# One projection of a hybrid decoder step: the prompt's mLSTM over five tiles, and six tiles as pairs

## The chip, the cores and the metric

The kernel runs on one core of a Trainium2 chip. A core has a matrix engine (TensorE, in the profile PE, with its weight loads as PEld), a vector engine (VectorE, DVE), a scalar engine (ScalarE, ACT), GpSimd (POOL) and a queue engine (SyncE, SP) that issues most of the transfers; POOL issues some as well. Matrix products go to PSUM, which has eight banks, and DVE or ACT must take them out. The metric is the device time of one execution in microseconds.

## What is computed

The reference is one inference step of a hybrid decoder layer. A prompt of 512 tokens and 32 sample tokens (8 sequences of 4), 544 columns in all, pass an input projection; an mLSTM branch and a windowed attention branch work side by side; each has its own output projection, gated; the sum goes through w_out and a layer norm with a residual. Cut to what matters here:

```python
q_m, k_m, v_m, o_m, z_m, q_a, k_a, v_a, z_a, g_m, g_a, i_pre, f_pre = split(x @ w_in)
# mLSTM of the prompt, 4 heads of 512: decays d from the gates, and
s = einsum('bhtd,bhsd->bhts', q, k) * d                  # cells
h = s @ v / max(|den|, exp(-m_row))                      # then a norm over the head, times the gates
C_new = decay * C + einsum('bhsk,bhsv->bhkv', w * k, v)  # keys: the new matrix memory, and n alike
# windowed attention with sinks gives the branch b_a, mLSTM the branch b_m (2048 wide each)
y = sigmoid(g_m) * (b_m @ w_proj_m) + sigmoid(g_a) * (b_a @ w_proj_a)
out = layernorm(alpha * x + y @ w_out)
```

All products are done at float32 accuracy in three products of rounded parts: a = ah + al, b = bh + bl, and ab is taken as ah bh + ah bl + al bh. The parts are made by `split` for weights (a cast on ACT to `wh`, a subtraction on DVE to `wl`) and `hilo` for activations (the same two steps, any tile).

## The kernel before

A projection of 2048 by 2048 is worked in 16 column tiles of 128. There are two forms.

*Plain tile* (`gemm`, matmuls on L210): the weights of a tile come in two halves of 8 x 128 x 128 (512 KB each), each half is split, and 2 x 8 x 3 matmuls of 128x272 for each of two banks, 96 in all, make the tile. After every `every`-th of the 16 row blocks `tick()` lets each live generator go one step, so that other work is put in the order between the matmuls: with `every=2` a tile holds 8 ticks. `drain()` runs what generators are left to their end.

*Pair* (`paired`, matmuls on L685 and L687): two column tiles as one product of 2 x 2 blocks with seven half products of 24 matmuls of 128x272 in place of eight (Strassen's scheme in Winograd's form). It needs sums of weight halves (`prepare`: DVE additions, or with `acc` two of them as transfers from POOL that accumulate) and sums of the activations' blocks (n2, s1, s4, n3), which must be there before the half product that uses them: half products 0 to 6 use, in this order, the plain left block, s1, n2, the low block, n3, s4, the low block again.

The program goes through these stages: the input projection in pairs (to 1757 us in the profiled execution), beside it attention and the sample tokens; the attention branch's projection w_proj_a, 16 plain tiles; w_proj_m as 4 plain tiles, 5 pairs, 2 plain tiles; w_out as 4 plain tiles, pairs and a tail with the layer norm.

The prompt's mLSTM stands beside w_proj_a. It is a generator (`mlstm`) of 20 steps a head for four heads. In a head: `values` (transposes of v on PE, `vh` by ACT, `vl` by DVE; four times), `decays` (one product, two copies and ten exponentials on ACT, spawned beside it), `keys` (transposes on L1425, a gated key on DVE at L1427, its parts `kwh` and `kwl`, then 24 products of 128x258 on L1438, and copies of C to the output on L1441 and L1442; four times), `cells` (scores on L1470, times decays on L1473, their parts, products on L1483, the norm), and the output (transposes on L1493, gate products on L1494, stores to `d_brm`). The parts of k are made on DVE (L1519 and L1520). At 8 ticks a tile the four heads take some ten tiles. When the generator has ended, `branch(d_brm)` reloads and splits the mLSTM branch over the remaining tiles.

`operand_sums` makes the four activation sums of a projection that is to be done in pairs: 8 steps, each with one transfer of 544 KB from POOL into one of two buffers `tx`, four sums on DVE (L1587 to L1590) and four `hilo`. It runs beside the four plain tiles of w_proj_m and of w_out.

What sets the order: each engine runs its instructions in the order in which the program leaves them, and waits at the first whose operands are not there. The program's order is that of the code, except that `tc.high_priority(offset=...)` moves work forward by so many instructions, that `tc.issue_after(x)` holds work behind instruction x, and that work whose buffers come free early may be placed early. Buffers come from pools with a fixed count: PSUM has the pools psB (tag sm, four banks: mLSTM and the other small work) and psA (tag bank, four banks: the tiles). The SBUF pools carry `reuse_waits="tile"`, so that memory given to a new pool waits for each old tile in it by itself.

## Time and profile before

| | |
|---|---|
| time, median of 3 executions | 2467.47 us (2466.90 to 2468.39) |
| the profiled execution | 2464.16 us, span 2462.4 us |
| PE busy | 2433.8 us (99%), 19446 matmuls |
| DVE busy | 1884.0 us (77%), 2813 instructions |
| ACT busy | 1215.4 us (49%) |
| POOL busy | 509.9 us (21%) |
| DMA | 464.72 MB, mean 189 GB/s |

Durations and counts are those of the profiled execution. A busy share is a mean over all stages. A group of instructions is a line, an engine, an operation and its tiles (out<-in), with the count, the busy time, the mean ns of one, and the time for which the engine was idle before them with what ended it. The durations of neighbouring instructions of one engine overlap, so one that reads 0.68 us can be started every 0.60 us. A line of the waits is engine, tile and line, what it waited for, the sum in us, the times and the longest.

### The profile page before, as it was taken

How to read it: one execution, taken by the hardware profiler on the slowest of the kernel's cores; microseconds unless marked ns; L12 is line 12 of the kernel's file. 1: busy time of each engine (PE TensorE's matmuls, PEld its weight loads, DVE VectorE, ACT ScalarE, POOL GpSimd, SP SyncE). 2: the span in 40 equal slices, each digit the busy share in tenths (PEclk: the TensorE clock that was granted, in tenths of full speed). 3: DMA queues.
4: the chain of work that ended last, by engine and by line, in shares of the span. 5: the costliest groups of instructions: out<-in, count | busy, mean ns of one | idle time of the engine just before them, and what ended most of it. 6: DMA issues, size and time to landing. Idle time of an engine off the chain costs nothing.

```text
span 2462.4 us, 48812 instructions
## 1 busy us (share of the span) xinstructions
PE 2433.8 (99%) x19446; PEld 2378.9 (97%) x19446; DVE 1884.0 (77%) x2813; ACT 1215.4 (49%) x1994; POOL 509.9 (21%) x478
## 2 busy tenths in 40 slices
PE   8999999999999999999999999999999999999997
PEld 8999999999999999999999999999999999999996
DVE  7768888888888887787887888878855654767657
ACT  5456676676676564433433444544633333344431
POOL 3114334334333331211121122210000000110111
PEclk9999999999999999999999999999999999999998
DMA  6866666666666644578587687576755546888876
GB/s 177 201 173 158 163 161 144 162 161 150 160 154 160 155 124 138 143 217 247 179 242 244 163 241 229 176 251 217 246 171 173 187 147 210 226 218 253 220 221 188
DMA packets 557436, 464.72 MB, mean 189 GB/s; under 512 B 45592, under 2 KB 454344, under 8 KB 556952
## 3 DMA queue, kind: packets, MB, share of 16 engines
q1 hardware_dynamic: 540312, 402.09, 55.1%
q0 software_dynamic: 15696, 57.15, 12.1%
q8 instruction: 153, 2.51, 0.4%
q10 hardware_dynamic: 1200, 2.36, 0.3%
q14 instruction: 75, 0.61, 0.1%
HBM read 319.06 MB, written 96.31 MB: 169 GB/s over the span
## 4 chain that ended last, share of the span: by engine, by line
PE 94%; DMA 3%; DVE 2%; issue 1%; ACT 1%; SPq 0%; DVEq 0%; POOL 0%; ACTq 0%; POOLq 0%
PE bank L685 46%; PE bank L687 23%; PE bank L210 11%; PE sm L1438 2%; PE sm L210 1%; PE bank L1250 1%; PE sm L1470 1%; PE sm L795 1%; PE sm L1483 1%; PE sm L841 1%; DMA tx<-d_y 1%; DMA ty<-d_y 1%; DMA raw<-in_w_in 1%; PE sm L1800 1%; PE sm L821 1%
## 5 line engine op out<-in xcount | busy, mean ns | idle before, releaser
L200 ACT CAST wh<-raw 128x1024 fp32r<-128x1024 f32 x632 | 662.7, 1049 | 836.2 <-PE bank L685 686.6
L201 DVE TENSOR_TENSOR wl<-raw,wh 128x1024 fp32r<-128x1024 f32 x632 | 792.2, 1255 | 194.6 <-ACT wh L200 175.3
L685 PE MATMUL bank<-xk,wh 128*128 128x272 f32 x2336 | 322.7, 289 | 0.0
L665 DVE TENSOR_TENSOR raw<-raw,raw 128x1024 f32<-128x1024 f32 x238 | 304.1, 1279 | 12.6 <-DMA raw<-in_w_in 8.3
L685 PEld LDWEIGHTS bank<-xk,wh 128*128 128x128 f32 x2336 | 303.0, 188 | 2.8 <-issue 2.4
L704 POOL TENSOR_TENSOR ev<-p,ev 128x272 f32<-128x272 f32 x82 | 117.9, 1438 | 458.3 <-ACT ev L703 401.2
L685 PE MATMUL bank<-n2h,wh 128*128 128x272 f32 x656 | 169.8, 291 | 0.2 <-ACT wh L200 0.2
L687 PE MATMUL bank<-xk,wl 128*128 128x272 f32 x1168 | 169.7, 288 | 0.0
L685 PE MATMUL bank<-n3h,wh 128*128 128x272 f32 x656 | 169.6, 291 | 0.0
L685 PE MATMUL bank<-s1h,wh 128*128 128x272 f32 x656 | 169.1, 291 | 0.0
L685 PE MATMUL bank<-n2l,wh 128*128 128x272 f32 x656 | 167.7, 288 | 0.0
L685 PE MATMUL bank<-n3l,wh 128*128 128x272 f32 x656 | 167.6, 288 | 0.0
L685 PE MATMUL bank<-s1l,wh 128*128 128x272 f32 x656 | 167.3, 287 | 0.0
L685 PE MATMUL bank<-s4h,wh 128*128 128x272 f32 x656 | 167.2, 289 | 0.0
L685 PE MATMUL bank<-s4l,wh 128*128 128x272 f32 x656 | 167.0, 287 | 0.0
L687 PEld LDWEIGHTS bank<-xk,wl 128*128 128x128 f32 x1168 | 155.6, 188 | 0.1
L685 PE MATMUL bank<-a11h,wh 128*128 128x272 f32 x584 | 150.6, 290 | 0.0
L685 PE MATMUL bank<-a11l,wh 128*128 128x272 f32 x584 | 149.4, 288 | 0.0
L210 PE MATMUL bank<-bh,wl 128*128 128x272 f32 x704 | 147.5, 290 | 0.7 <-DVE wl L201 0.7
L210 PE MATMUL bank<-bh,wh 128*128 128x272 f32 x704 | 148.1, 289 | 0.0
L210 PE MATMUL bank<-bl,wh 128*128 128x272 f32 x704 | 148.0, 289 | 0.0
L663 POOL DMA_DIRECT2D raw<-raw x90 | 78.1, 868 | 291.8 <-DVE ev L712 202.2
(493 smaller groups left out, 5670.4 us busy)
## 6 DMA issues: line engine op xcount, KB each, us to landing
raw<-in_w_in SPq DMA_DIRECT2D x296, 512.0 KB
raw<-raw POOLq DMA_DIRECT2D x90, 512.0 KB, 4.8
C<-in_state_mlstm_C SPq DMA_DIRECT2D x32, 1024.0 KB
out<-C SPq DMA_DIRECT2D x64, 512.0 KB
raw<-in_w_proj_a SPq DMA_DIRECT2D x32, 512.0 KB
raw<-in_w_proj_m SPq DMA_DIRECT2D x32, 512.0 KB
raw<-in_w_out SPq DMA_DIRECT2D x32, 512.0 KB
d_v<-ev SPq DMA_DIRECT2D x16, 272.0 KB
```

The lines of the kernel that those rows point to most:

```text
L200: state["cast"] = A.copy(wh[:, k:k + n], raw[:, k:k + n])
L201: state["split"] = V.tensor_tensor(out=wl[:, k:k + n], in0=raw[:, k:k + n], in1=r32(wh[:, k:k + n]), op=ALU.subtract)
L210: PE.matmul(ps[f][:, :w], a[:, kk], b(k, c, w), start=(k == 0 and n == 0), stop=(k == 15 and n == 2))
L663: G.dma_start(out=w[out][:], in_=w[b][:], accum_op=ALU.add)
L665: V.tensor_tensor(out=w[out][:], in0=w[a][:], in1=w[b][:], op=ALU.add)
L685: PE.matmul(ps, wh[:, k], x(p, k), start=(first and k == 0 and p == 0), stop=False, skip_group_check=True)
L687: state["end"] = PE.matmul(ps, wl[:, k], x(0, k), start=False, stop=(k == 7), skip_group_check=True)
L704: G.tensor_tensor(out=c22, in0=p1, in1=c11, op=ALU.subtract)
L795: PE.matmul(pp[:, c0 + w0:c0 + 256], qs[a][:, j * 128:j * 128 + 128], kx[:, k0:k0 + 256 - w0], start=(n == 0), stop=(n == 1))
L821: PE.transpose(pt[:, b * 128:b * 128 + 128], s_[:, b, 128:256], ident)
L841: PE.matmul(po[:, b * 128:b * 128 + n], VA[:, b], p_[:, 2 * b:2 * b + n // 128], start=(b == 0 and m == 0), stop=(b == 3 and m == 1), skip ...
L1438: PE.matmul(pp[:, 0:258], a[:, b * 128:b * 128 + 128], b_[:, b, f], start=(b == 0 and n == 0), stop=(b == 3 and n == 2))
```

## The change

The line numbers of the new kernel differ: `gemm`'s matmuls are L216 there, the pairs' L691 and L693, `split` L206 and L207, `hilo` L251 and L252, the keys' transposes L1437, the gated key L1439, the keys' products L1450, the copies of C L1453 and L1454, scores L1482, the cells' products L1498, transposes and gate products of the output L1512 and L1513, the plain tile's eviction L1621, the loads of sums L1583 and L1584, the sums L1594 to L1600.

- The attention branch's projection has five plain tiles with the mLSTM beside them (`LEAD_A`), then three plain tiles with the operand sums of this branch beside them, then three pairs (tiles 8 to 13), then two plain tiles with `branch(d_brm)`.
- In the five tiles a half has other tick counts (`every=(1, 2)`: 12 ticks a tile), and the tiles' work is held behind the last matmul of the mLSTM put down so far (`behind_cells`). The mLSTM has 15 steps a head: the loads of k and v of the next head come a head earlier, the parts of q are made between the keys, and the output of a head (`rows_out`) is a generator of its own that runs beside the next head.
- The casts of k go from DVE to ACT (`two_parts` with `hilo`), and so does the second half of the copy of C.
- The PSUM pools also have `reuse_waits="tile"` and can be closed: six banks for sm and two for bank from the lead stage to the pairs, four and four before and after.
- `operand_sums` works in two passes of 8 steps, first n2 and s1, then s4 and n3, with two transfers a step (272 KB and 136 KB) into one of three buffers `tx`. All three projections use it; `rest` puts what is left of it ahead of the fifth half product of the first pair.

```diff
             kw["side"] = side or "right"
+        if space is not bass.MemoryType.DRAM:
             kw["reuse_waits"] = "tile"
...
+    esPS = ExitStack()
+    es.callback(esPS.close)
+
+    def psum_pools(n):
+        return pool(esPS, nm("psB"), n, PSUM), pool(esPS, nm("psA"), 8 - n, PSUM)
...
-            products(ps, half, wh, wl, xh, xl, cols, every)
+            products(ps, half, wh, wl, xh, xl, cols, every[half] if isinstance(every, tuple) else every)
...
-    def paired(work, plain=None):
+    def paired(work, plain=None, rest=()):
...
+            if at == 4:
+                for _ in rest:
+                    pass
...
+    esPS.close()
+    psB, psA = psum_pools(6)
...
-                    PE.matmul(pp[:, 0:258], a[:, b * 128:b * 128 + 128], b_[:, b, f],
+                    state["cells"] = PE.matmul(pp[:, 0:258], a[:, b * 128:b * 128 + 128], b_[:, b, f],
...
-        V.tensor_copy(co[:, 256:512], p1[:, 0:256])
+        A.copy(co[:, 256:512], p1[:, 0:256])
...
+        if h + 1 < MH:
+            pre["v"] = load4(d_v, h + 1)
+        gt = load4(d_g, h)
...
-            yield
-        gt = load4(d_g, h)
+            if js[-1] == 3 and h + 1 < MH:
+                pre["k"] = load4(d_k, h + 1)
+            yield
+        spawn(rows_out(h, hns, gt))
+
+    def rows_out(h, hns, gt):
         for c in range(4):
...
+        pre = {"v": load4(d_v, 0), "k": load4(d_k, 0)}
         for h in range(MH):
-            vts = load4(d_v, h)
+            vts, kts = pre["v"], pre["k"]
             spawn(decays(h))
-            yield
-            kts = load4(d_k, h)
             for c in range(4):
                 yield from values(h, c, vts[c])
             qts = load4(d_q, h)
             kh, kl, qh, ql = [], [], [], []
+
+            def two_parts(src, to):
+                a, b_ = t5(F32R), t5(F32R)
+                hilo(src[:], a[:], b_[:])
+                for tiles, t_ in zip(to, (a, b_)):
+                    tiles.append(t_)
+
             g_ = None
             for c in range(4):
-                a, b_ = t5(F32R), t5(F32R)
-                V.tensor_copy(a[:], kts[c][:])
-                V.tensor_tensor(out=b_[:], in0=kts[c][:], in1=r32(a[:]), op=ALU.subtract)
-                kh.append(a)
-                kl.append(b_)
+                two_parts(kts[c], (kh, kl))
                 n_ = keys(h, c, kts[c])
                 next(n_)
+                if c > 1:
+                    two_parts(qts[c - 2], (qh, ql))
                 if g_ is not None:
                     for _ in g_:
                         pass
                 g_ = n_
                 yield
-            for c in range(4):
-                a, b_ = t5(F32R), t5(F32R)
-                hilo(qts[c][:], a[:], b_[:])
-                qh.append(a)
-                ql.append(b_)
+            for c in (2, 3):
+                two_parts(qts[c], (qh, ql))
             for _ in g_:
                 pass
             yield
-            yield from cells(h, kh, kl, qh, ql)
+            yield from cells(h, kh, kl, qh, ql, pre)
...
+    def operand_sums(src, to, p, pace=1):
+        f, e = ([[p.tile([128, 4, 2, HT], F32R, tag="act", name=nm("sum" + n)) for _ in range(2)] for n in "hl"]
+                for _ in range(2))
+        to["n2"], to["s1"], to["s4"], to["n3"] = (
+            (lambda q, k, t=t, j=j: t[q][k // 4][:, k % 4, j]) for t in (e, f) for j in range(2))
+
+        def load(n):
+            k, c = n % 8, slice(HT, T) if n < 8 else slice(0, HT)
+            t_ = tx.tile([128, 3, HT], F32, tag="tx", name=nm("tx"))
+            G.dma_start(out=t_[:, 0:2].rearrange("p c t -> p (c t)"), in_=src[k])
+            G.dma_start(out=t_[:, 2], in_=src[k + 8][:, c])
+            return t_
+
+        ahead = [load(n) for n in range(3)]
+        for n in range(16):
+            for _ in range(pace if n < 12 else 1):
+                yield
+            k, t_ = n % 8, ahead.pop(0)
+            u, v, w = (t_[:, j] for j in range(3))
+            if n < 8:
+                V.tensor_tensor(out=v, in0=w, in1=v, op=ALU.subtract)
+                V.tensor_tensor(out=u, in0=u, in1=v, op=ALU.subtract)
+                to_ = e
+            else:
+                V.scalar_tensor_tensor(v, u, -1.0, v, op0=ALU.mult, op1=ALU.subtract)
+                V.tensor_tensor(out=u, in0=w, in1=r32(to["n2"](0, k)), op=ALU.subtract)
+                V.tensor_tensor(out=u, in0=u, in1=r32(to["n2"](1, k)), op=ALU.subtract)
+                to_ = f
+            hilo(t_[:, 0:2], *(t[k // 4][:, k % 4] for t in to_))
+            if n + 3 < 16:
+                ahead.append(load(n + 3))
...
+    def plain_a(ct, **kw):
         sg = c5t()
-        nc.sync.dma_start(sg[:], d_sga[ct])
-        ps = gemm(wa_, ct * 128, bah, bal, every=2)
+        with tc.issue_after(state["load"].ins):
+            nc.sync.dma_start(sg[:], d_sga[ct])
+        ps = gemm(wa_, ct * 128, bah, bal, **kw)
...
+        return dict(wv=wa_, x=XA, cA=ct * 128, cB=ct * 128 + 128, scale=1.0, acc=True, end=end, early=early)
+
+    LEAD_A, PAIR_A, TAIL_A = 5, 8, 14
+    def behind_cells():
+        return tc.issue_after(state["cells"].ins) if "cells" in state else ExitStack()
+
+    for ct in range(LEAD_A):
+        with behind_cells():
+            plain_a(ct, every=(1, 2))
     drain()
-    def operand_sums(src, to, p):
-
-        def load(k):
-            t_ = tx.tile([128, 2, T], F32, tag="tx", name=nm("tx"))
-            G.dma_start(out=t_[:], in_=src[k:k + 9:8].rearrange("k p t -> p k t"))
-            return t_
-
-        ahead = [load(0), load(1)]
-        for k in range(8):
-            for _ in range(2):
-                yield
-            t_ = ahead.pop(0)
-            r11, r21, r12, r22 = (t_[:, a, c:c + HT] for a in range(2) for c in (0, HT))
-            V.tensor_tensor(out=r22, in0=r22, in1=r21, op=ALU.subtract)
-            V.scalar_tensor_tensor(r21, r11, -1.0, r21, op0=ALU.mult, op1=ALU.subtract)
-            V.tensor_tensor(out=r11, in0=r11, in1=r22, op=ALU.subtract)
-            V.tensor_tensor(out=r12, in0=r12, in1=r11, op=ALU.subtract)
-            for name, r_ in (("s1", r22), ("n2", r11), ("n3", r21), ("s4", r12)):
-                if name not in to:
-                    to[name] = quad(p, name)
-                hilo(r_, to[name][0][:, k], to[name][1][:, k])
-            if k < 6:
-                ahead.append(load(k + 2))
-
-    def operands(tiles, sums):
-
-        low = [t[2:] for t in tiles]
-        return [side_by_side(tiles, 0), quarter(sums["s1"]), quarter(sums["n2"]), side_by_side(low, 0),
-                quarter(sums["n3"]), quarter(sums["s4"]), side_by_side(low, HT)]
-
-    def c6t():
-        return c6.tile([128, T], F32, tag="c6", name=nm("c6"))
+    esA.close()
+    es3, esE = ExitStack(), ExitStack()
+    act3 = pool(es3, "act3", 8)
+    c6 = pool(esE, "c6", 2)
+    esR = ExitStack()
+    wr2, pe_ = pool(esR, "wr2b", 3), pool(esR, "peb", 1)
+    tx = pool(esR, "txb", 3)
+    SA = {}
+    sums_ = operand_sums(d_bra, SA, act3, 2)
+    next(sums_)
+    spawn(sums_)
+    for ct in range(LEAD_A, PAIR_A):
+        with behind_cells():
+            plain_a(ct, every=2, prio=AHEAD)
+    esPS.close()
+    psB, psA = psum_pools(4)
+    XA = operands((bah_, bal_), SA)
+    paired([pair_a(ct) for ct in range(PAIR_A, TAIL_A, 2)], state["split"], rest=sums_)
+    state["end"] = None
+    drain()
+    bm_, bmh, bml, g_ = branch(d_brm, act3, lambda k: ev() if k % 5 < 3 else c6t())
+    spawn(g_)
+    for ct in range(TAIL_A, 16):
+        plain_a(ct, every=2, prio=AHEAD)
...
-    spawn(operand_sums(d_brm, M, act))
+    sums_ = operand_sums(d_brm, M, act)
+    next(sums_)
+    spawn(sums_)
```

## The prediction

> **What bounds the kernel now.** I read the page's busy table and slices first, then the windows of the stages that the change touches, then PE's own waits and the chain.

> ```profile
> span 2462.4 us, 48812 instructions
> PE 2433.8 (99%) x19446; PEld 2378.9 (97%) x19446; DVE 1884.0 (77%) x2813; ACT 1215.4 (49%) x1994; POOL 509.9 (21%) x478
> PE   8999999999999999999999999999999999999997
> ...
> 1740.00:1760.00 20.00, 19.30 (x154) 19.08 (x153) 16.02 (x22) 13.97 (x21) 1.47 (x1) 1.00 1.01 332
> 1760.00:1780.00 20.00, 20.00 (x165) 19.95 (x164) 18.70 (x31) 14.99 (x30) 0.21 (x2) 1.00 0.81 262
> 1780.00:1800.00 20.00, 20.00 (x153) 19.53 (x153) 7.57 (x16) 3.90 (x8) 0.00 (x0) 1.00 0.35 111
> 2020.00:2120.00 100.00, 100.00 (x804) 100.00 (x803) 58.40 (x104) 36.88 (x62) 4.35 (x6) 1.00 0.74 225
> ...
> PE bank L210 <- DVE wl L201: 1.5, 2, 0.7
> ...
> 2014.15 111.71 PE bank L210 x895
> ```

> The columns of a window are its length, the busy time of PE, PEld, DVE, ACT and POOL, the granted clock, the DMA share and GB/s. PE is dense: its only wait from 1757 to 2400 is one of 0.70 us (the waits list it twice). So PE's work sets the time: work taken from PE is gained in full, and every wait that PE gets is paid in full. DVE has idle time on average, but at the start of the first mLSTM head (1760 to 1780) it is busy 18.70 of 20 us and ACT 14.99. This is the stage that the change compresses.

> **The sum's base.** The profiled execution took 2464.16 us (span 2462.4), 3.3 us below the median 2467.47. I sum against it and add 3.3 at the end.

> **What PE loses.** Six tiles of the projection become three pairs, with seven half products of 24 matmuls each where two tiles had eight: 3 x 24 = 72 matmuls of 128x272 go, and all other PE work stays. The chain's row gives 111.71 / 895 = 0.1248 us for one, so PE has 9.0 us less work: -9.0.

> **What is packed.** The same mLSTM now stands beside five tiles, not ten, so some 60 us less of matmuls cover it, and the operand sums of this branch are new work. I counted PE's work through the new order of instructions, in us t from the first product of w_proj_a (t = 0 is 1757.7 in this trace), and laid DVE's and ACT's queues beside it in their new order, with these durations:

> ```profile
> L201 DVE TENSOR_TENSOR wl<-raw,wh 128x1024 fp32r<-128x1024 f32 x21 | 25.6, 1218 | 4.8 <-ACT wh L200 4.7
> L200 ACT CAST wh<-raw 128x1024 fp32r<-128x1024 f32 x21 | 22.1, 1050 | 19.4 <-issue 12.8 <-PE bank L210 6.5
> L1427 DVE TENSOR_TENSOR f<-sm,colT 128x512 f32<-128x512 f32 x16 | 10.9, 684 | 0.1
> L246 DVE TENSOR_TENSOR kwl<-f,kwh 128x512 fp32r<-128x512 f32 x16 | 10.9, 686 | 3.6 <-ACT kwh L245 3.6
> L1494 DVE TENSOR_TENSOR t<-sm,t 128x512 f32<-128x512 f32 x16 | 10.2, 683 | 16.5 <-PE sm L1493 16.5
> L245 ACT CAST kwh<-f 128x512 fp32r<-128x512 f32 x16 | 9.9, 620 | 20.8 <-DVE f L1427 20.7
> L1442 DVE COPY f<-sm 128x256 f32<-128x256 f32 x16 | 6.8, 422 | 24.1 <-PE sm L1438 24.1
> L1519 DVE CAST t<-t 128x512 fp32r<-128x512 f32 x16 | 6.7, 420 | 1.5 <-DMA t<-d_k 1.5
> L1560 DVE TENSOR_TENSOR c<-bank,c 128x272 f32<-128x272 f32 x20 | 7.9, 429 | 2.5 <-PE bank L210 2.3
> ...
> 1766.12 1.55 ACT L245 CAST vh<-sm 128x512 fp32r<-128x512 f32 x3
> 1768.08 1.28 ACT L1458 ACT_TABLE_LOAD   x1
> 1769.37 3.04 ACT L1458 ACTIVATE dm<-f,colT 128x128 f32<-128x128 f32 x10
> 1774.77 1.29 ACT L245 CAST kwh<-f 128x512 fp32r<-128x512 f32 x2
> ...
> 1827.02 0.78 DVE L1560 TENSOR_TENSOR c<-bank,c 128x272 f32<-128x272 f32 x2
> 1827.71 1.22 DVE L201 TENSOR_TENSOR wl<-raw,wh 128x1024 fp32r<-128x1024 f32 x1
> 1828.84 1.28 DVE L1494 TENSOR_TENSOR t<-sm,t 128x512 f32<-128x512 f32 x2
> ...
> 1777.65 0.40 PE L1438 MATMUL sm<-vh,kwh 128*128 128x258 f32 x2
> ```

> The groups' fields are busy us and the mean ns of one. In a row of the timeline, x2 in 1.28 us where one lasts 0.68 says that a queue without gaps starts a 512-column DVE operation every 0.60 us; likewise 0.35 for a 272-column eviction, 1.13 for a split of a weight half (1827.71 to 1828.84), and on ACT 0.30 for an exp and 0.50 for a cast of 512 columns (x3 in 1.55 us).

> What left DVE is counted: 16 casts of k (0.42) and 16 copies of half of C (0.42) go to ACT, 13.4 us in all. ACT can take them on average; at head 0 its queue is the long one.

> *Head 0.* PE reaches the products of the keys (old L1438) at t = 14.3. Before kwh, ACT must do, from t = 7.2, four casts of vh and three first parts of k (3.5), the split of a weight half (1.0), the copy of a 384-column tile (0.5), the table load (1.3), ten exps (3.0) and the cast of kwh itself (0.6); with 0.1 at each change of form 10.5 us, so kwh stands at 17.7. The trace of before shows the same date: the first of two casts that start at 1774.77 ends at 1775.4 = t 17.7, and there PE asked only at 1777.65. Wait: 3.4 us and 0.3 for the second part: +3.7. The first three steps of sums stand in DVE's order here and wait for loads on POOL; if these are late they add up to 4; I take nothing, as they are issued about ten us ahead.

> *Head 1.* Ask at t = 56.8. DVE has seven operations of 512 columns (two vl, one k part, three gate products, then the gated key) from 53.2 on, 4.2 us, and ACT's cast 0.6: kwh at 58.0, 1.2 us late. The second block's kwh then lacks another 1.25, and its kwl, queued behind a weight split of 1.13, another 1.2: +3.7.

> *Head 2.* The tile ends at t = 97.7. DVE then owes two evictions (0.70), three gate products, two vl and the gated key (3.6) without a gap, and ACT a cast: kwh at 102.7 where PE asks at 99.4, +3.4. Then a weight split (1.13), a gate product, three low parts, the second gated key and kwl, 4.7 us, while PE can go on for 0.5 us in place of them: +3.5. Together +6.9.

> *Head 3.* Matmuls of a tile stand between its parts: nothing.

> The ends of these terms: none at all if the order of before's margins survives (there PE never waited), and twice, 28 us, if each late part delays the next head's too. I take the queue's sum, 14.3, because head 0's date is read directly from a row.

> **Tiles 5 to 7 on two banks.** Six banks go to mLSTM in the lead stage, two to the tiles, and these three are still built so. A new tile's first matmul waits for the eviction of the one before: 0.43 and its start, against 0.12 of cover, so about 0.5 at each boundary. At the end of tile 5 the evictions stand behind three low parts of sums (0.63 each): 1.5. Sum +2.1; bounds 1 and 4.

> **The sums of the attention branch.** Sixteen steps, each with two loads on POOL, three buffers.

> ```profile
> tx<-d_brm POOLq DMA_DIRECT2D x2, 544.0 KB, 8.2
> ...
> L1578 POOL DMA_DIRECT2D tx<-d_y x8: 722/722/1055, 2218.5 to 2294.3; - x8
> DMA to landing us min/median/max: 3.9/6.3/9.0
> ...
> 2254.86 0.41 PE L210 MATMUL bank<-yh,wh 128*128 128x272 f32 x2
> ...
> 2278.95 14.23 DMA tx<-d_y x2
> L246 DVE TENSOR_TENSOR s4l<-tx,s4h x8: 429/434/441, 2264.8 to 2302.5; 128x272 fp32r<-128x272 f32 x8
> ```

> A step costs 2 x 0.72 on POOL, a landing (5 us for 408 KB, nearer the lower half of 3.9 to 9.0 for 544 KB) and about 2.3 on DVE and ACT: 8.7 / 3 = 2.9 us. Thirteen steps after the lead stage take 38, and tiles 5 to 7 with the first four half products give 35.6 + 12 = 47.6 less the wait for free buffers at their start and the paced first twelve steps. The last four steps are emitted ahead of the fifth half product and end within about 5 us of its need: 0 to 5, I take 2.0. Sums of the next branch that DVE meets in pair 1 before their load lands: 0 to 4, I take 0.8. The two later stages do 16 steps where they did 8: for w_out the old last part ended at 2302.5, when its four tiles did (2254.9 + 4 x 96 x 0.1248 = 2302.8), so it was tight; sixteen steps from 2261 on end at 2307, and the second pass is wanted only at the fifth half product, 12 us after the tiles: 0, at most 5 (below). POOL's 96 loads in place of 16 add 58 us to 510 of 2462: off the path. The three pairs' additions of weight halves (DVE, and six DMAs with accumulation) repeat what the stage before 1757 does with PE dense. DMA traffic grows by some 11 MB on 465.

> **The sum.** -9.0 + 3.7 + 3.7 + 6.9 + 2.1 + 2.0 + 0.8 = +10.2: 2474.4 for an execution like the profiled one, 2477.7 as the median.

> [...] This trace shows what a wait of PE may cost beyond itself:

> ```profile
> PE sm L328 <- ACT a21h L245: 3.0, 1, 3.0
> ...
> 12.00:13.00 1.00, 0.00 (x0) 0.91 1.03 383
> 13.00:14.00 1.00, 0.61 (x3) 0.50 1.04 384
> 15.00:16.00 1.00, 1.00 (x6) 0.50 1.22 307
> 17.00:18.00 1.00, 1.00 (x10) 1.00 1.05 384
> ```

> (PE busy, granted clock, DMA share, GB/s.) After a gap of 3.0 us the clock was 0.50 from 12.9 to 16.1, some 3 us of work at half speed: 1.5 us more. [...] In the sum I charge nothing: the tail's clock fell only 3.9 us after the last matmul,

> ```profile
> 2446.00:2448.00 2.00, 0.01 (x1) 1.00 1.03 396
> 2448.00:2450.00 2.00, 0.00 (x0) 0.98 1.03 396
> 2450.00:2452.00 2.00, 0.00 (x0) 0.50 0.36 99
> ```

> which is longer than my waits (0.3 to 3.4 at a stretch).

> **Rivals.** *PE stays dense.* Keys' parts at heads 0 to 2 come in time, as in before, where the same operations left PE no wait; the time is 2464.2 - 9.0 + 3.3 = 2458.5, faster. For it: DVE idles half of 1780 to 1800, and loads of k and v come a head earlier now. Against it: the 1775.4 of head 0. It decides where all waits together stay below 4.1 us (9.0 less the 4.9 of 0.2%). Chance 0.20.
> *Waits of half my size* (DVE's backlog at heads 1 and 2 partly worked off while PE waits at head 0): about +9.6 in place of 19.2: 2468, no change. 0.14.
> *The clock falls* at the four waits of over 3 us: 4 x 1.5 = +6: 2483.7. 0.08; speaks against it the tail's 3.9 us.
> *The sums' loads land late*, at 8.2 as beside the old lead stage: a step is (8.2 + 1.4 + 2.3) / 3 = 4.0 us, and DVE, waiting for a load, holds weight splits behind it: thirteen steps take 52, +4.5; w_out's sixteen 64 against 47.6 + 12, +5; less the 2.8 already charged: 2484.4. 0.08.
> Forecast 0.50, within 2469 to 2485.

> **Numbers.** About 0.2%, 4.9 us, is what a measurement of this kernel tells from no change. Faster: the dense case and a little of the half one, 0.23; same 0.14, mostly the half case; slower 0.63. The range 2460 to 2488 leaves out most of the dense case and the sum of two bad ones.

> **What would show it.** PE with 19446 - 72 = 19374 matmuls. In the waits of PE, products of keys (new L1450) waiting for ACT kwh and DVE kwl, some 14 us in six to eight pieces, at heads 0 to 2 and none at head 3; new L216 waiting for evictions (L1621) at tiles 6 and 7; pairs waiting for sums, 0 to 5 us. Windows of 20 us at the heads' starts with DVE near 20 and PE at 16 to 18. I am wrong if the keys never wait (then the sum is -9 and the queue arithmetic failed), or if PE waits on loads of sums in the pairs or at w_out for more than 5 us.

## The result, and the profile after

The changed kernel takes 2498.65 us (median, 2498.41 to 2499.54) against 2467.18 us: ratio 1.0128, 95% interval 1.011 to 1.0145, or 31.5 us slower. The forecast was slower by 10, with 2488 as the upper end. Its profiled execution has a span of 2496.6 us, 34.2 more than the one before. The page's busy table of the changed kernel:

```profile
span 2496.6 us, 48978 instructions
PE 2437.0 (98%) x19374; PEld 2376.2 (95%) x19374; DVE 1922.5 (77%) x2842; ACT 1244.5 (50%) x2028; POOL 564.8 (23%) x567
```

PE has the 72 matmuls less (19374), yet it is busy 3 us longer, and it idles 31 us more: 2496.6 - 2437.0 against 2462.4 - 2433.8. Most of PE's waits are in two stretches: from 1757 to 1960, the heads of the mLSTM, and from 1960 to 2050, the tiles with the sums and the first pair. The longest of each:

```profile
PE sm L1450 <- ACT kwh L251: 5.1, 5, 2.4
PE sm L1450 <- DVE kwl L252: 3.8, 2, 3.3
PE sm L1429 <- DMA t<-d_v: 2.3, 1, 2.3
PE sm L1450 <- issue: 1.1, 1, 1.1
...
PE bank L691 <- ACT sumh L251: 3.4, 2, 1.9
PE bank L691 <- DVE suml L252: 2.2, 1, 2.2
PE bank L216 <- DVE c L1621: 1.9, 1, 1.9
```

Where the time went can be read from the starts of equal half products. First, of the kernel before, the first matmul of w_proj_a and the half product with s1 of the first pair of w_proj_m; then, of the changed kernel, the same first matmul and the half product with s1 of its pairs 1, 2 and 3 and of the first pair of w_proj_m:

```profile
1757.08 0.41 PE L210 MATMUL bank<-bh,wh 128*128 128x272 f32 x2
...
2128.71 0.29 PE L685 MATMUL bank<-s1h,wh 128*128 128x272 f32 x1
```

```profile
1757.08 0.41 PE L216 MATMUL bank<-bh,wh 128*128 128x272 f32 x2
...
2007.72 0.36 PE L691 MATMUL bank<-sumh,wh 128*128 128x272 f32 x1 [1.34 <-DVE c L1621]
...
2040.62 0.29 PE L691 MATMUL bank<-sumh,wh 128*128 128x272 f32 x1
...
2061.68 0.28 PE L691 MATMUL bank<-sumh,wh 128*128 128x272 f32 x1
...
2160.54 0.28 PE L691 MATMUL bank<-sumh,wh 128*128 128x272 f32 x1
```

Before, 371.6 us lie between; less 1944 matmuls of 0.1248 us, 129.0 are left for the mLSTM's own PE work and one wait of 0.7. With that and the same rate, the changed kernel should pass the first three marks after 227.8, 21.0 and 21.0 us, and the last after 92.9. It took 250.6, 32.9, 21.1 and 98.9: lost 22.8 us in the heads and the tiles up to pair 1, 11.9 in pair 1, nothing in pair 2, 6.0 in pair 3, two tiles and w_proj_m's four. With 2.7 more to the last matmul these make 43.4 us, and less the 9.0 of the matmuls 34.4.

Some of that is the clock. Columns: length, PE busy, granted clock, DMA share, GB/s.

```profile
1870.00:1880.00 10.00, 4.27 (x23) 3.65 (x22) 9.91 (x17) 5.00 (x9) 0.00 (x0) 0.72 0.71 235
1880.00:1890.00 10.00, 10.00 (x81) 10.00 (x80) 4.34 (x8) 3.15 (x7) 0.00 (x0) 0.94 0.34 105
...
2020.00:2030.00 10.00, 4.13 (x21) 3.23 (x21) 5.81 (x12) 1.80 (x4) 3.23 (x6) 0.73 1.01 279
2030.00:2040.00 10.00, 10.00 (x63) 9.88 (x62) 8.30 (x15) 3.68 (x4) 1.97 (x3) 0.76 0.39 101
```

(These rows have the busy times of PE, PEld, DVE, ACT and POOL ahead of the clock.) At 1870 to 1880 DVE is busy 9.91 of 10 us while PE works 4.27: the head's start that the forecast named. Busy time multiplied by what the clock lacks, summed over windows of 1 us, is 1.9 us there, 3.2 in pair 1 and 1.5 in pair 3: 6.6 us. A further part is the edges of the waits. In dense work a matmul of a tile starts 0.125 us after the one before; the last one before a wait runs its 0.29 us to the end, and the first one after a wait is followed only 0.20 to 0.23 us later, so a wait costs some 0.26 us beside itself. So the 22.8 us up to pair 1 come out, within half a us: 17.6 us of idle time in 14 waits, less the 0.7 of before, 1.9 of clock, and edges of 3.8 us, summed over the 14.

### The profile page after: what moved, and what is told of

Same layout as the page of the kernel before. It is cut to its first block, busy times and chain, and to the rows that moved or that the text cites. A ratio compares the mean times of both kernels' runs of the same rounds, so it can differ in the third digit from the quotient of the medians.

```text
span 2496.6 us, 48978 instructions
## 1 busy us (share of the span) xinstructions
PE 2437.0 (98%) x19374; PEld 2376.2 (95%) x19374; DVE 1922.5 (77%) x2842; ACT 1244.5 (50%) x2028; POOL 564.8 (23%) x567
## 5 line engine op out<-in xcount | busy, mean ns | idle before, releaser
L206 ACT CAST wh<-raw 128x1024 fp32r<-128x1024 f32 x641 | 671.8, 1048 | 819.0 <-PE bank L691 686.0
L207 DVE TENSOR_TENSOR wl<-raw,wh 128x1024 fp32r<-128x1024 f32 x641 | 803.5, 1255 | 180.4 <-ACT wh L206 159.9
L691 PE MATMUL bank<-xk,wh 128*128 128x272 f32 x2336 | 322.7, 289 | 0.0
L691 PEld LDWEIGHTS bank<-xk,wh 128*128 128x128 f32 x2336 | 303.0, 188 | 2.9 <-issue 2.4
L693 PE MATMUL bank<-xk,wl 128*128 128x272 f32 x1168 | 169.7, 287 | 0.0
L693 PEld LDWEIGHTS bank<-xk,wl 128*128 128x128 f32 x1168 | 155.6, 188 | 0.1
L691 PE MATMUL bank<-n2h,wh 128*128 128x272 f32 x584 | 151.3, 291 | 1.4 <-ACT wh L206 1.4
L691 PE MATMUL bank<-n3h,wh 128*128 128x272 f32 x584 | 151.1, 291 | 0.1
L691 PE MATMUL bank<-s1h,wh 128*128 128x272 f32 x584 | 150.7, 291 | 0.0
L691 PE MATMUL bank<-a11h,wh 128*128 128x272 f32 x584 | 150.6, 290 | 0.0
L691 PE MATMUL bank<-a11l,wh 128*128 128x272 f32 x584 | 149.4, 288 | 0.0
L691 PE MATMUL bank<-n2l,wh 128*128 128x272 f32 x584 | 149.3, 287 | 0.0
L691 PE MATMUL bank<-n3l,wh 128*128 128x272 f32 x584 | 149.2, 287 | 0.0
L691 PE MATMUL bank<-s1l,wh 128*128 128x272 f32 x584 | 148.9, 287 | 0.0
L691 PE MATMUL bank<-s4h,wh 128*128 128x272 f32 x584 | 148.8, 288 | 0.0
L691 PE MATMUL bank<-s4l,wh 128*128 128x272 f32 x584 | 148.5, 287 | 0.0
L216 PE MATMUL bank<-bh,wh 128*128 128x272 f32 x512 | 110.3, 290 | 2.9 <-DVE c L1621 1.9
L691 PEld LDWEIGHTS bank<-n2h,wh 128*128 128x128 f32 x584 | 109.9, 188 | 2.6 <-ACT wh L206 1.9
L691 PEld LDWEIGHTS bank<-n3h,wh 128*128 128x128 f32 x584 | 109.8, 188 | 1.9 <-issue 1.7
```

The source lines that it names most:

```text
L206: state["cast"] = A.copy(wh[:, k:k + n], raw[:, k:k + n])
L207: state["split"] = V.tensor_tensor(out=wl[:, k:k + n], in0=raw[:, k:k + n], in1=r32(wh[:, k:k + n]), op=ALU.subtract)
L216: PE.matmul(ps[f][:, :w], a[:, kk], b(k, c, w), start=(k == 0 and n == 0), stop=(k == 15 and n == 2))
L691: PE.matmul(ps, wh[:, k], x(p, k), start=(first and k == 0 and p == 0), stop=False, skip_group_check=True)
L693: state["end"] = PE.matmul(ps, wl[:, k], x(0, k), start=False, stop=(k == 7), skip_group_check=True)
```

## The experiments

**The theory** after the first profile: three separate causes. The heads' first parts stand in DVE's and ACT's queues (the forecast's step); the sums of the attention branch are late for pair 1 (underestimated); casts of the mLSTM branch stand too early in ACT's queue (not seen). The rival: the pairs, six banks or the new order inside a head cost by themselves. All ratios below are to the kernel before on the same chip; the changed kernel again gave 1.0129 (1.0112 to 1.0146).

> The changed kernel unchanged, on the chip of the next three, as their base: ratio to before 1.011 to 1.0145 as first measured, with the same waits within 1 us at each head.

It repeated: 13.7 us at the heads, with the wait for v at 3.1 in place of 2.3.

**Packing without pairs.**

```diff
-    LEAD_A, PAIR_A, TAIL_A = 5, 8, 14
+    LEAD_A, PAIR_A, TAIL_A = 5, 14, 14
...
-    sums_ = operand_sums(d_bra, SA, act3, 2)
...
-    paired([pair_a(ct) for ct in range(PAIR_A, TAIL_A, 2)], state["split"], rest=sums_)
```

> The changed kernel without its three pairs and without the sums of the attention branch: nine plain tiles follow the five packed ones; PE's work is that of before. Theory A (the queues of DVE and ACT at the starts of the heads cost what the packing costs, independently of the pairs): the waits from 1757 to 1920 stay, 13.4 us idle in after, with about 1.6 us of half clock and 2.5 us of matmul drain, and w_proj_m and w_out keep their waits for sums, about 6 us; the pairs' share goes: 2467.2 + 17.5 + 6 to 7 = 2491 to 2492. Theory B (the pairs and their sums bring the waits, the packed heads are hidden): within 3 us of before, 2468 to 2474.

1.0143 (1.0128 to 1.0159): theory B fell, and A's size too. The waits of PE in the whole stretch:

```profile
PE sm L1450 <- ACT kwh L251: 10.3, 5, 4.2
PE bank L216 <- DVE c L1621: 7.1, 9, 2.0
```

The packing alone costs 35 us, 11 more than expected: 7.1 at the nine boundaries of tiles on two banks, and the heads wait longer than in the changed kernel, where the order of their instructions is not quite the same. The longest of these waits, 4.2 us at head 1, begins with a store: DVE's gated key waited 5.0 us until `out<-f`, a copy of C, had freed its buffer (1.2 us in the changed kernel). The wait for v is gone, as no loads of sums stand beside it. So the pairs are not what makes the kernel slow, and a kernel that differs in its order cannot be subtracted to a microsecond.

**Seven tiles beside the mLSTM.**

```diff
-    LEAD_A, PAIR_A, TAIL_A = 5, 8, 14
+    LEAD_A, PAIR_A, TAIL_A = 7, 10, 14
...
-            plain_a(ct, every=(1, 2))
+            plain_a(ct, every=2 if ct else (1, 2))
```

> Seven tiles beside the mLSTM in place of five (12 ticks in the first, 8 in the others), three tiles with sums, then two pairs and two tiles: 24 us more of matmuls cover the heads, PE has 24 matmuls (3.0 us) more than in after. Theory A (cover): the heads' waits fall from 13.4 to under 4 us and their half clock goes, -11 to -13, +3.0 for the pair given up: 2488 to 2491. Rival (the waits come from the new order inside a head, tiles held behind the cells and six banks, whatever the number of tiles): heads' waits of 11 to 14 us again, time 2499 to 2503.

1.0102 (1.0087 to 1.0118), 2488.89 us, the time that theory A gave (its interval just meets that of the changed kernel). The waits at the heads fell from 12.7 us to 6.5, not under 4: head 0 kept its 2.4 for v and 1.4 for the keys. **Six tiles**, with four banks from the mLSTM's end and four tiles for the sums, did not follow it:

```diff
-    LEAD_A, PAIR_A, TAIL_A = 5, 8, 14
+    LEAD_A, PAIR_A, TAIL_A = 6, 10, 14
...
-            plain_a(ct, every=(1, 2))
+            plain_a(ct, every=2 if ct > 2 else (1, 2))
     drain()
+    esPS.close()
+    psB, psA = psum_pools(4)
...
```

> Six tiles beside the mLSTM (12, 12, 12, 8, 8, 8 ticks), four with the sums, two pairs, two tiles, and four PSUM banks for the tiles again as soon as the mLSTM has ended: PE has 24 matmuls more than after (+3.0). Theory (heads short of cover; sums late for pair 1; two banks let evictions behind sums stop the tiles): heads' waits 8 to 10 in place of 12.7, pair 1 without waits, tile boundaries under 1 us: -10 to -14, ratio 1.007 to 1.009. Rival (sums and weight splits share DVE's queue, and the wait moves wherever they meet): ratio 1.011 to 1.013, as in the run with five tiles for the sums.

1.0125 (1.0108 to 1.0142): the theory's numbers fell, and the time lies in the rival's range. Pair 1 had one wait of 3.3 us, for a weight split on DVE; the heads kept theirs. The windows of heads 1 and 2 (1820 to 1900) tell why; in order the changed kernel, six tiles, seven tiles, and eight tiles (below):

```profile
1820.00:1900.00 80.00, 71.08 (x526) 0.96 0.44 147
```

```profile
1820.00:1900.00 80.00, 70.52 (x534) 0.96 0.46 152
```

```profile
1820.00:1900.00 80.00, 78.12 (x606) 0.98 0.53 171
```

```profile
1820.00:1900.00 80.00, 79.95 (x641) 1.00 0.57 189
```

With six tiles the first three still have 12 ticks, so heads 1 and 2 are as dense as before, and PE idles 9 us there as in the changed kernel. At 8 ticks a tile it idles 1.9 us or nothing. At heads 1 and 2 not the number of tiles but the ticks beside each head decide. Head 0 is another matter: with 8 ticks in every tile it still waits 3.0 us for v and 1.5 for the keys.

**Which queue, and the banks.** First the casts of k go back to DVE:

```diff
-            def two_parts(src, to):
+            def two_parts(src, to, eng=A.copy):
...
-                hilo(src[:], a[:], b_[:])
+                eng(a[:], src[:])
+                V.tensor_tensor(out=b_[:], in0=src[:], in1=r32(a[:]), op=ALU.subtract)
...
-                two_parts(kts[c], (kh, kl))
+                two_parts(kts[c], (kh, kl), V.tensor_copy)
```

> After with the first parts of k cast on DVE again (16 casts of 0.42 us, as before) in place of ACT. Queue theory: DVE's queue at heads 1 to 3 is the one that makes PE wait, so each head's waits for kwh and kwl grow by the casts that stand ahead (two to four, 0.35 us each): +2 to +5 us, ratio 1.0138 to 1.015. Rival (ACT's queue with the exps sets the heads): heads 0 and 1 get shorter, ratio 1.010 to 1.0125.

1.0142 (1.0127 to 1.0157), in the theory's range, though the interval meets that of the changed kernel. The waits moved: kwh 8.0 us in place of 5.1 to 5.8 in the changed kernel and its repeats, kwl 2.3 in place of 3.8.

```profile
PE sm L1450 <- ACT kwh L251: 8.0, 6, 2.7
PE sm L1450 <- DVE kwl L252: 2.3, 2, 2.0
```

Together they are 10.3 us, where the changed kernel has 10.0 with the 1.1 that its list puts down to "issue". So this run does not settle which of the two queues sets the heads.

The other edit gives the mLSTM four banks in place of six:

```diff
-    psB, psA = psum_pools(6)
+    psB, psA = psum_pools(4)
```

> After with four and four PSUM banks in the lead stage and in tiles 5 to 7, as before. Theory: the two-bank boundaries go (1.9 us at tile 6 and parts of 1.0 at tile 7 and 1.3 at the pairs), the heads' waits are set by DVE's and ACT's queues and stay within 3 us of 12.7: -1 to -4, ratio 1.011 to 1.0125. Rival (six banks are what lets the heads' small work run ahead): waits for sm banks appear at the heads, +3 to +10, ratio 1.014 to 1.017.

1.017 (1.0155 to 1.0185): the rival was right. With four banks for the mLSTM, its products also wait for banks, most of all the cells' products for the norm on ACT:

```profile
PE sm L1498 <- ACT t L1085: 2.7, 1, 2.7
```

So the six banks are worth more than the boundaries that they cost.

**The loads of v.**

```diff
-    next(sums_)
+    with tc.issue_after(state["pool"].ins):
+        next(sums_)
```

(`state["pool"]` is the mLSTM's last instruction on POOL.)

> After with the first three steps' loads of sums held behind the last GpSimd instruction of the mLSTM (in after POOL issues them at 1752 to 1757, beside the loads of v, with the DMA engines at 1.08). Theory: PE's wait for the load of v (2.3 to 3.1 us at 1761) goes, and half of it comes back as the keys of head 0 are then bound by ACT (they were ready at t = 17.7): -1 to -3, ratio 1.0115 to 1.0125. Rival (the loads of v are late by themselves): the wait stays, and the later sums cost pair 1 up to 3 us more: ratio 1.0125 to 1.0145.

1.0145 (1.013 to 1.016). The wait for v is gone, so the early loads of sums had made it. The time is in the rival's range, not clear of the changed kernel's, and pair 1 takes back what head 0 saves:

```profile
PE bank L691 <- DVE suml L252: 5.7, 3, 3.2
```

**The casts of the mLSTM branch.** In the changed kernel, ACT's timeline in pair 3, and PE behind it:

```profile
2066.89 1.05 ACT L206 CAST wh<-raw 128x1024 fp32r<-128x1024 f32 x1 [0.35 <-PE bank L691]
2074.09 0.64 ACT L251 CAST bh<-ev 128x544 fp32r<-128x544 f32 x1 [6.14 <-DMA ev<-d_brm]
...
2076.28 0.59 PE L691 MATMUL bank<-sumh,wh 128*128 128x272 f32 x1 [2.40 <-ACT wh L206]
```

```diff
     paired([pair_a(ct) for ct in range(PAIR_A, TAIL_A, 2)], state["split"], rest=sums_)
-    state["end"] = None
     drain()
...
         plain_a(ct, every=2, prio=AHEAD)
     drain()
+    state["end"] = None
```

> The steps that split the mLSTM branch are held behind the last half product of the pairs (in after ACT meets two of their casts inside the third pair and sits 6.1 us for their loads, and a weight split behind them makes PE wait 2.4 us at 2074 and lose the clock for 3.3 us). Theory: that wait and its half clock go, -4: 2494 to 2495. Rival: the casts are then late for tile 14, which needs the whole branch, and PE waits there as long or longer: 2498 to 2504.

This edit put the hold on PE's instructions alone, and those steps have none: the order of every engine stayed as it was. It is a second repeat (1.0136, 1.0121 to 1.0151). Held behind ACT's last cast of a weight half, for this branch alone (`hold`):

```diff
-                hilo(st[:], hs[k // 4][:, k % 4], los[k // 4][:, k % 4])
+                with tc.issue_after(state["cast"].ins) if hold else ExitStack():
+                    hilo(st[:], hs[k // 4][:, k % 4], los[k // 4][:, k % 4])
```

> After with ACT's casts of the mLSTM branch held behind the weight splits of the last pair (holding the steps behind a matmul, the edit tried first, left every engine's order as it was). In after two of them stand inside the third pair, wait 5 to 6 us for their loads, and PE then waits 1.9 to 2.4 us for a weight split, in one profile of two with 3.3 us of half clock behind it. Theory: that wait goes and nothing takes its place, since w_proj_m, which needs the branch, is 24 us away: -2 to -4, ratio 1.0113 to 1.012. Rival (the loads themselves are late): the wait moves to the first tile of w_proj_m, ratio 1.0125 to 1.014.

1.0123 (1.0108 to 1.0138). By time alone it can't be told from the changed kernel; by the trace the cause is plain. Windows 2060 to 2160 of the changed kernel and of this one:

```profile
2060.00:2160.00 100.00, 96.28 (x755) 0.98 0.86 259
```

```profile
2060.00:2160.00 100.00, 100.00 (x801) 1.00 0.91 270
```

All of PE's waits in pair 3, the two tiles and w_proj_m's four came from the branch's early casts: some 4 us of idle time and a fall of the clock. Part of the gain was met by longer waits in pair 1 (3.3 us for one low part) and by a new one of 1.7 us in w_proj_m's first pair.

**The sums.** With five tiles beside them:

```diff
-    LEAD_A, PAIR_A, TAIL_A = 5, 8, 14
+    LEAD_A, PAIR_A, TAIL_A = 5, 10, 14
```

> After with five tiles beside the sums of the attention branch in place of three, then two pairs and two tiles: PE has 24 matmuls more (+3.0). Theory (the sums start when the mLSTM's memory is free, at 1976, and take 4.1 us a step, 53 us for 13 steps, so their end at 2030 is late for three tiles and early enough for five): the waits of the first pair (11.9 us with their half clock) go: -9, ratio 1.009 to 1.010. Rival (the waits of the pairs come from sums and their loads meeting weight splits in DVE's and POOL's queues, wherever they stand): the waits move to the five tiles or stay in pair 1, ratio 1.013 to 1.015.

1.0117 (1.0102 to 1.0132), between theory and rival: pair 1 no longer waits, but the tiles' boundaries do, since with two banks an eviction behind sums in DVE's queue stops PE.

```profile
PE bank L216 <- DVE c L1621: 7.4, 4, 2.8
```

The same pairs, fed with plain blocks in the places of the sums, show what the sums cost. This kernel leaves the sums and their loads out and so computes something else; its matmuls are as many:

```diff
...
-    XA = operands((bah_, bal_), SA)
+    lowa = [t[2:] for t in (bah_, bal_)]
+    XA = [side_by_side((bah_, bal_), 0), side_by_side((bah_, bal_), HT), side_by_side(lowa, HT), side_by_side(lowa, 0),
+          side_by_side((bah_, bal_), HT), side_by_side(lowa, 0), side_by_side(lowa, HT)]
...
```

> After without the operand sums of the attention branch: the three pairs are fed with plain blocks of the branch in the places of n2, s1, s4 and n3, so they compute something else; every matmul, weight addition and transfer of weights stays, only the 16 steps of sums with their 32 loads are left out. Theory (the sums cost the stage after the heads what it lost): waits between 1960 and 2080 fall from about 14 us to 4 (two-bank boundaries and the branch's casts), the wait for v at head 0 goes with the early loads: -13 to -17, ratio 1.006 to 1.008. Rival (the pairs' own additions and loads, right behind plain tiles, are the cost): -2 to -5, ratio 1.011 to 1.012.

1.0073 (1.0056 to 1.0089), 2483.51 us, in the theory's range and clear of 1.0112. Windows 2000 to 2060 of the changed kernel and of this one:

```profile
2000.00:2060.00 60.00, 51.37 (x375) 0.91 0.75 202
```

```profile
2000.00:2060.00 60.00, 60.00 (x482) 1.00 0.72 179
```

The pairs themselves run dense. Their sums cost (1.0129 - 1.0073) x 2465 = 13.8 us, some 6 either way by the two intervals; the spans of the profiles differ by 14.3. That is more than the 9.0 that three pairs save. The sums of the two later stages cost little by themselves. The kernel before with the new `operand_sums`:

```diff
-            tx = pool(esR, "txb", 2)
+            tx = pool(esR, "txb", 3)
...
-    spawn(operand_sums(d_brm, M, act))
+    sums_ = operand_sums(d_brm, M, act)
+    next(sums_)
+    spawn(sums_)
...
-    tx = pool(esT, "txd", 2)
+    tx = pool(esT, "txd", 3)
```

> The kernel before with only the operand sums changed: two passes of eight steps, two loads a step, three buffers, in w_proj_m and w_out. Theory A: DVE's queue meets sums whose loads have not landed, with weight splits behind them, as in after (waits of 2.9 us in w_proj_m and 3.4 us in w_out): +5 to +8, 2472 to 2475. Rival: those waits come from what precedes them in after (late branch, late stores), and alone the new sums are hidden as the old ones were: 2466 to 2469.

1.001 (1.0 to 1.0019), 2.5 us: less than the theory's 5 to 8 and near the rival, by which the new sums are hidden; one wait of 2.2 us in w_out's first pair.

**The clock.**

```diff
+                if h == 2 and c == 0 and b == 0 and n == 1:
+                    for _ in range(12):
+                        state["cells"] = PE.matmul(pt[:, 0:258], kwh[:, 0:128], vh[:, 0, 0], start=True, stop=True)
```

> After, with twelve products of 128x258 more (1.45 us of PE, their result is not used) put between the fourth and the fifth keys product of head 2, where PE waited 2.38, did four products and waited 3.34 us for kwl. Clock theory: with work between the two waits the granted clock stays at 1.00 from 1870 to 1885 (in after 0.50 from 1874.7 to 1881.1, of which PE worked 3.2 us), the wait for kwl shrinks by the 1.45 us and the time by 1.6 us: ratio about 0.0006 under after. Rival (the clock falls by itself at a wait of such length, or costs nothing): clock 0.50 again after 1874 and the time as after, or up to 1.45 us longer.

1.0131 (1.0115 to 1.0146), no gain. The clock fell though PE worked between the waits:

```profile
1876.82 0.51 PE L1450 MATMUL sm<-vh,kwh 128*128 128x258 f32 x2 [2.39 <-ACT kwh L251]
...
1877.41 2.71 PE L1454 MATMUL sm<-vh,kwh 128*128 128x258 f32 x12
```

```profile
1876.00:1877.00 1.00, 0.18 (x1) 1.00 0.53 201
1877.00:1878.00 1.00, 1.00 (x8) 0.74 0.61 186
1878.00:1879.00 1.00, 1.00 (x6) 0.50 0.58 175
1883.00:1884.00 1.00, 1.00 (x6) 0.50 0.00 0
1884.00:1885.00 1.00, 1.00 (x9) 0.84 0.00 0
```

The twelve products, 1.45 us at full clock (0.12 us apiece, as L1450's from 1779 to 1783 in the changed kernel), took 2.7. One wait of 2.4 us stands before the fall, and the clock stayed at half for 6.8 us, from 1877.5 to 1884.3.

**All together.** Seven tiles, four banks after the mLSTM, held casts (the edit as above); then, on top of it, eight tiles and one pair:

```diff
-    LEAD_A, PAIR_A, TAIL_A = 5, 8, 14
+    LEAD_A, PAIR_A, TAIL_A = 7, 10, 14
...
-            plain_a(ct, every=(1, 2))
+            plain_a(ct, every=2 if ct else (1, 2))
     drain()
+    esPS.close()
+    psB, psA = psum_pools(4)
     esA.close()
```

> The run with seven tiles beside the mLSTM (ratio 1.0102), with four banks for the tiles again when the mLSTM has ended and with the branch's casts held. If the mechanisms add up: boundaries -2, casts and their half clock -2 to -4, the rest (heads about 7, sums about 8 with clock, w_proj_m and w_out 5, against 6 saved) stays: ratio 1.0080 to 1.0092. If waits only move: 1.0095 to 1.0110.

```diff
-    LEAD_A, PAIR_A, TAIL_A = 7, 10, 14
+    LEAD_A, PAIR_A, TAIL_A = 8, 12, 14
...
-            plain_a(ct, every=2 if ct else (1, 2))
+            plain_a(ct, every=2)
```

> Eight tiles at 8 ticks each beside the mLSTM, four tiles beside the sums, one pair, two tiles; banks and casts as in the run before. PE saves 24 matmuls (3.0 us) against before. Theory (tick density decides at the heads, cover decides at the sums): heads 4 to 6 with the wait for v, pair without waits, sums 2 to 4, w_proj_m and w_out 3 to 5: +6 to +12 net of the 3.0, ratio 1.0025 to 1.005. Rival (the new order inside a head and the six banks cost by themselves): ratio 1.007 or more.

1.009 (1.0075 to 1.0106) and 1.0035 (1.0024 to 1.0045), both as expected. No version here beats the kernel before: the fewer ticks stand beside a head and the more tiles beside the sums, the nearer the time comes to it, while the pairs left to save PE time run out.

## Why the prediction was wrong

The forecast gave +10.2 us on the profiled execution, and the marks above give 34.4. Of the 24.2 between them, 9.1 are pair 1 (11.9 in place of 2.8), 6.4 the stretch up to it (22.8 in place of 16.4), 6.0 pair 3 to w_proj_m's first pair and 2.7 what follows, both charged with nothing.

*What bounds it, and the nine microseconds*: right. PE has 19374 matmuls, and where nothing else disturbs it (pair 2, or the pairs without sums) a pair passes in 21.0 us.

*The heads*: right in place, and in cause and size at heads 1 to 3. Forecast 14.3 us: head 0 3.7, head 1 3.7, head 2 6.9, head 3 none. Measured: 3.8, 2.9, 6.0 and none, 12.7 us of waits. PE's timeline of the changed kernel, the longest of them:

```profile
1763.06 0.66 PE L1429 MATMUL sm<-cc,t 128*128 128x128 f32 x4 [2.34 <-DMA t<-d_v]
1776.79 0.48 PE L1450 MATMUL sm<-vh,kwh 128*128 128x258 f32 x2 [1.14 <-issue]
...
1822.93 0.51 PE L1450 MATMUL sm<-vh,kwh 128*128 128x258 f32 x2 [1.05 <-ACT kwh L251]
...
1873.44 0.51 PE L1450 MATMUL sm<-vh,kwh 128*128 128x258 f32 x2 [2.38 <-ACT kwh L251]
...
1877.53 0.80 PE L1450 MATMUL sm<-vh,kwl 128*128 128x258 f32 x2 [3.34 <-DVE kwl L252]
```

Head 2's pair of waits, 2.38 and 3.34, stands where the queues put 3.4 and 3.5. At head 0 the agreement is luck: 2.3 of the 3.8 us are the wait for v, and the keys cost 1.4. Their kwh came at t = 19.6, not 17.7, but the waits ahead of it had already put PE back by 3.0. In the two runs above without that wait (loads held; no sums) head 0's keys cost 2.3 and 3.4. The wait for v was not forecast: the prediction feared that the sums' early loads would land late, and they made another load late.

*Two banks*: 2.1 forecast; 1.9 and 1.3 at the boundaries where PE waited for an eviction behind sums in DVE's queue, and 1.0 at the third, where it waited for a weight cast that stood behind two casts of sums on ACT. The cause was right and the size half of it.

*The sums*: this step failed, both in the time of a step and in the start. It charged 2.0 + 0.8, from 2.9 us a step and 38 us for thirteen, counted from the end of the lead stage; a wait for free buffers at the start was named there without a price. ACT's first casts of sums, transfers and queue of the changed kernel, 1955 to 2040:

```profile
1974.75 1.74 ACT L251 CAST sumh<-tx 128x544 fp32r<-128x544 f32 x3 [3.85 <-DMA d_brm<-t]
1976.45 0.58 POOL L1583 DMA_DIRECT2D tx<-d_bra  x1 [11.80 <-DVE suml L252]
...
tx<-d_bra POOLq DMA_DIRECT2D x13, 272.0 KB, 4.4
tx<-d_bra POOLq DMA_DIRECT2D x13, 136.0 KB, 5.4
...
POOL tx L1583: 42.3, 10
```

The landing was as assumed (4.4 and 5.4 us). But the lead stage's last tile ended at 1962.3, and ACT could cast the first sums only at 1974.75, after a store of the mLSTM (`d_brm<-t`), whose memory the new tiles take. So the loads that refill the buffers began only at 1976.45, when DVE had made the first low parts: one of the three covering tiles was over by then. POOL then waited 42.3 us in ten pieces for DVE to free a buffer. Thirteen steps took from 1976.5 to 2030, 4.1 us each, so with three buffers one goes round in 12.3 us, where the prediction had 8.7. Of these, 1.1 are the issue (1.4 forecast), about 5 the landing (5), and so about 6 the queues of DVE and ACT, for which 2.3 were charged: that is a step's own work, and it stands there among splits, evictions and other steps. Pair 1 lost 11.9 us where 2.8 were charged, 5.6 of it in waits for parts of sums (more than 5 for loads of sums was a sign that the prediction had named itself), and the sums as a whole cost 13.8. The rival "the sums' loads land late" had 4.0 us a step and the place, from a wrong cause.

*The clock*: charged with nothing, on the tail's 3.9 us after the last matmul; 6.6 us were lost. This step failed too: the tail shows a fall 3.9 us after the last matmul, and the prediction read that as how long PE has to wait to cause one. The other row of the prediction, 0.50 after a gap of 3.0 us, was the better guide: the changed kernel's trace has falls at waits of 2.4 us amid dense work (2.38 us at head 2, 2.40 in pair 3). The rival that charged four falls, 6 us, was right in size.

*The branch's casts* were missing from the sum: reordered to stand inside pair 3, they made PE wait there and in w_proj_m (a row of 100.00 of 100 with these casts held back, 96.28 in the changed kernel).

So both slower rivals came true at once in size, each priced on its own and given 8 in 100. The edges of the waits, 0.26 us each and 3.8 up to pair 1, were in no sum.

## What to carry to other kernels

Before packing work beside fewer matmuls, lay every engine's queue in its new order beside PE's dates: that gave the waits at heads 1 to 3 within 1 us each. Do the same for each buffer ring: its period is load, queue of the consumer and release together, and the consumer's queue was about half of it here. A gain of 9 us of matmuls is gone as soon as the operands that allow it cost 14 in a queue that PE depends on, and waits of a dense PE like those of 2.4 us here are to be priced with the half clock that can stand behind them: three stretches of 3.4 to 10.2 us at 0.50 cost the changed kernel 6.6 us (the next section has them).

## What the runs showed of the hardware

```profile
1874.00:1875.00 1.00, 0.18 (x2) 0.71 0.73 108
1875.00:1876.00 1.00, 0.00 (x0) 0.50 0.98 308
...
1880.00:1881.00 1.00, 1.00 (x7) 0.50 0.00 0
1881.00:1882.00 1.00, 1.00 (x9) 0.88 0.00 0
...
2024.00:2025.00 1.00, 0.43 (x2) 0.80 0.85 253
2025.00:2026.00 1.00, 0.00 (x0) 0.50 1.17 323
...
2034.00:2035.00 1.00, 1.00 (x7) 0.58 0.06 16
2035.00:2036.00 1.00, 1.00 (x10) 1.00 0.00 0
...
2075.00:2076.00 1.00, 0.00 (x0) 0.90 0.66 168
2076.00:2077.00 1.00, 0.72 (x3) 0.50 1.12 319
...
2079.00:2080.00 1.00, 1.00 (x9) 0.89 0.42 161
2080.00:2081.00 1.00, 1.00 (x10) 1.00 0.00 0
```

Not each such wait did it: of the profiles of kernels that wait 2.2 to 3.3 us for v at head 0, some show 1.00 there and some 0.91 in a window of 20 us. Waits of one length gave both. Here are the wait for v and the window of the changed kernel's repeat, and the same of the run with twelve products:

```profile
PE sm L1429 <- DMA t<-d_v: 3.1, 1, 3.1
...
1760.00:1780.00 20.00, 15.69 (x127) 1.00 0.94 310
```

```profile
PE sm L1429 <- DMA t<-d_v: 3.1, 1, 3.1
...
1760.00:1780.00 20.00, 16.14 (x117) 0.91 1.00 321
```

With a wait of 2.3 us the changed kernel has 1.00 there, and the run with five tiles beside the sums 0.91. So the length of a wait alone does not tell whether the clock falls; what else decides it was not shown.
